# The values' part of the removals in one burst with the first corner product, its copies behind the corner copies

## The chip, the cores and the metric

One of the eight cores of a Trainium2 chip runs the whole program, and the metric is the device time of one execution in microseconds (us); lower is better. The core has a matrix engine (TensorE, PE in the profile, with its weight loads as PEld), VectorE (DVE), ScalarE (ACT) and GpSimd (POOL), each working through its own list of instructions in order, and SyncE (SP), whose list here is the DMA transfers that it issues. TensorE writes its results to banks of PSUM, from which the other engines read them.

## The reference

One step of a bidirectional hybrid layer on 128 context tokens and 256 latent tokens with 2048 channels. A normalised input is projected by `w_in`, 20,864 columns wide. One branch is an RWKV-7 time mixing in 32 heads of 64 channels, with a scan in each direction; the other a gated short convolution; both are projected, gated, merged and projected again. The scan, for each head and direction:

```python
def step(S, inp):
    r_t, w_t, k_t, v_t, a_t, b_t = inp
    sa = jnp.einsum('dbhij,dbhj->dbhi', S, a_t)
    S = S * w_t[..., None, :] + sa[..., :, None] * b_t[..., None, :] + v_t[..., :, None] * k_t[..., None, :]
    y = jnp.einsum('dbhij,dbhj->dbhi', S, r_t)
    return S, y
```

`sa` is the removal: what the state S gives for the key `a_t`, written back along `b_t` in the same step. The values `v_t` of earlier steps are in S too, and so they have a part in every later removal.

## The kernel before

**The stream.** `Stream` multiplies the input by the columns of `w_in`, 128 or 256 at a time. All matmuls are in a 32-bit format of reduced precision; to keep float32, each operand is split in a high and a low part, and a product is three matmuls (`mm3`, lines 81 to 83). A step of the stream is one `mm3` of 128 x 384. Weights come in loads of 1 MB on SyncE (`raw_*`, two buffers); from each, ScalarE casts two high parts (`whi_*`, line 88) and VectorE subtracts for two low parts (`wlo_*`, line 89), three buffers each. A load waits until the `wlo` of the load two before it is done. `ds_.go(n)` issues n steps.

**The blocks.** The scan runs in 16 blocks `b` of two heads. Each direction has six chunks of 64 tokens, so a block has 12 chunk products `f`, each for two heads `h`. A block is prepared and scanned while the stream goes on: every `yield n` in a preparing or scanning function is followed by n stream steps (`drive`). TensorE's order is thus written out by hand (`manual_schedule`). The other engines' lists are ordered by the scheduler, by estimated times and priorities: the scan has priority 300, all else 0.

**A block in order.** `prep_b` makes the score matrices on TensorE (`pA`), masks them into `A`, and sends the 32 x 32 diagonal blocks of the removals by DMA (`ui`) into `U`, where VectorE inverts them in 30 dependent pairs of steps (lines 721 and 723, about 29 us). ScalarE makes the transpose `UT` (line 727). `U` and `UT` go out to DRAM (`uo`, lines 728 and 729) and come back as blocks of `A` (line 734, four transfers) and as `x11` (line 735, two transfers, `x` in the profile). `prep_c` transposes values (`pv`) and keys (`pb`) and, at its end, computes `pav`: 24 products of 64 x 64, on TensorE as 48 passes, of the values in `sav[64:128]` with `A[64:128]`. ScalarE copies the two banks to `sav[0:64]` in four copies, and POOL clears `A[64:128, 0]` behind the products. Then `prep_a` of the next block loads two small weights (`lraw`, one buffer, line 621), splits them (`lwh` on ScalarE, `lwl` on VectorE, one buffer each), and multiplies by them (`pl`, four times) with stream steps between; `pn` is a product with two matmuls. At least 80 stream steps (`WINDOW`) after the start of `prep_c` the scan begins.

**The scan.** `corner("pH")` is 24 products of 32 x 32 (48 passes) of `A` and `x11`, copied back to `x11[32:64]` by ScalarE and VectorE in turn. `chain(1)` and `chain(0)` are the recurrences: `po` (state by scores), added onto `sav` on VectorE; `pq`, copied to `sav[0:64]` by ScalarE; `pu`, added to the state `st` by VectorE. `corner("pX")` is the second corner, copied to `A[0:32]`. `prep_k` of the next block is held back behind those copies by `issue_after`, which makes the scheduler put what is in its scope behind a given instruction. `py` is the output product.

**Banks.** `pl`, `pn`, `pav`, `pH`, `pX` and the recurrences share five PSUM banks in turn (`bank`). The stream has three of its own.

In the profile's names the numbers are left out: `wlo_bg` is a low weight part of the group `bg`, `d_bg` its result bank.

Of the kernel before, what the change touches and what calls it, by code (L numbers as in the profile page):

```python
# [15 lines left out]
P = 128  # L16
# [5 lines left out]
C = 64  # L22
NCH = 6
# [33 lines left out]
def hybrid_step(ctx, tc, cst, x_prompt, x_sample, state_f, state_b, c, c_ctx, ada_w, ada_b, norm_g,  # L57
# [3 lines left out]
    V, S, G, TE = nc.vector, nc.scalar, nc.gpsimd, nc.tensor  # L61
# [191 lines left out]
    def pcol(i, n=1):  # L253
        return par[:, i:i + n]
# [154 lines left out]
    def tmp(nm):  # L409
        return box["sp"].tile([P, T], F32, tag="t", name=nm, bufs=8)  # L410
# [177 lines left out]
    hss = [slice(0, C), slice(C, P)]  # L588

    def bank(nm):  # L590
        return ps1.tile([P, 4, P], F32, tag="A", name=nm, bufs=5)
# [4 lines left out]
    def flat(a):  # L596
        return a.rearrange("p n t -> p (n t)")
# [4 lines left out]
    def hl_parts(t, hi, nm):  # L602
        lo = sp.tile([P, T], F32R, tag="t", name=f"lo_{nm}", bufs=8)
        S.copy(hi[:], t[:])
        V.tensor_tensor(lo[:], t[:], hi[:].bitcast(F32), ALU.subtract)
        return hi, lo
# [130 lines left out]
    def prep_c(b, o):  # L737

        r, v, A = r_[b], v_[b], o["A"]

        s_in = sp.tile([P, 2, C], F32, tag="s_in", name=f"s_in_{b}")
        for d in range(2):
            for h in range(2):
                for jb in range(2):
                    p0 = C * h + 32 * jb
                    nc.sync.dma_start(s_in[p0:p0 + 32, d, :].rearrange("i (b j) -> i b j", j=32),
                                      ctx_st[d][0, 0, 2 * b + h].rearrange("(b i) j -> i b j", i=32)
                                      [:, :, 32 * jb:32 * jb + 32])

        sav = sp.tile([P, 2 * NCH, P], F32, tag="sav", name=f"sav_{b}")  # L750
        bt = sp.tile([P, 2 * NCH, P], F32, tag="bt", name=f"bt_{b}")
        o["sav"], o["bkt"] = sav, bt
        for d in range(2):
            if d == 0:
                src = v
            else:
                src = tmp(f"vr_{b}")
                S.copy(src[:], v[:, ::-1])
            pv = bank(f"pv_{b}_{d}")
            for q in range(3):  # L760
                TE.transpose(pv[:, q, :], src[:, q * P:(q + 1) * P], ident)
            for e in range(2):
                S.copy(sav[C:P, NCH * d + e:NCH * d + NCH:2, :], pv[C * e:C * e + C, 0:3, :])
            yield 1
        for d in range(2):

            for n0, n1 in (((0, 4), (4, 5)), ((0, 3), (4, 6)))[d]:
                pb = bank(f"pb_{b}_{d}_{n0}")
                for n in range(n0, n1):
                    TE.transpose(pb[:, n - n0, :], o["bk"][d][:, n, :], ident)  # L770
                S.copy(bt[:, NCH * d + n0:NCH * d + n1, :], pb[:, 0:n1 - n0, :])
                yield 1
        pvs = [bank(f"pav_{b}_{d}") for d in range(2)]
        for f in range(2 * NCH):
            for h in range(2):
                TE.matmul(flat(pvs[f // NCH][hss[h]])[:, C * (f % NCH):C * (f % NCH) + C], A[C:P, 0, f, hss[h]],
                          sav[C:P, f, hss[h]], start=True, stop=True)
        for d in range(2):
            for h in range(2):
                S.copy(sav[0:C, NCH * d:NCH * d + NCH, hss[h]],  # L780
                       flat(pvs[d][hss[h]])[:, 0:NCH * C].rearrange("p (n i) -> p n i", i=C))

        G.memset(A[C:P, 0, :, :], 0.0)
        yield 2
        ks = o["kd"]
        V.tensor_tensor(ks[0][:], ks[0][:], ks[1][:, ::-1], ALU.add)
        V.scalar_tensor_tensor(ks[0][:], ks[0][:], pcol(RK + b), r[:], ALU.mult, ALU.mult)
        o["bsum"] = hl_parts(ks[0], sp.tile([P, T], F32R, tag="t", name=f"bsh_{b}", bufs=8), f"bs_{b}")
        yield 1
        for h in range(2):  # L790
            for d in range(2):
                V.transpose(st[1][hss[h], d, hss[h]], s_in[hss[h], d, :])

    def scan(b, o):
        A, x11, sav, bt = o["A"], o["x11"], o["sav"], o["bkt"]
# [51 lines left out]
        def corner(nm, lhs, rhs):  # L847
            pz = bank(f"{nm}_{b}")
            for f in range(2 * NCH):
                for h in range(2):  # L850
                    g = 32 * (2 * (f % 2) + h)
                    TE.matmul(flat(pz[g:g + 32])[:, 32 * (f // 2):32 * (f // 2) + 32], lhs(f, h), rhs(f, h),
                              start=True, stop=True)
            return [flat(pz[32 * j:32 * j + 32])[:, 0:192].rearrange("p (n t) -> p n t", t=32) for j in range(4)]

        pz = corner("pH", lambda f, h: A[0:32, 0, f, C * h + 32:C * h + C], lambda f, h: x11[0:32, 2 * f + h, :])
        for j in range(4):
            (S.copy, V.tensor_copy)[j % 2](x11[32:64, j::4, :], pz[j])
        yield H0
        lat = chain(1)  # L860
        next(lat)
# [9 lines left out]
        pz = corner("pX", lambda f, h: x11[32:64, 2 * f + h, :], lambda f, h: A[32:64, 0, f, C * h + 32:C * h + C])  # L871
# [16 lines left out]
        for q in range(3):  # L888
            for h in range(2):
                for d in range(2):  # L890
                    for e in range(2):
                        f = 2 * q + e if d == 0 else NCH + 5 - 2 * q - e
                        TE.matmul(py[hss[e], q, hss[h]], A[:, 1, f, hss[h]], sav[:, f, hss[h]],
                                  start=d == 0, stop=d == 1)
# [43 lines left out]
    def drive(gen, prio=0, at=None, fn=None):  # L938
        n = i = 0
        while True:  # L940
            if i == at:
                fn()
            i += 1
            with tc.high_priority(offset=prio):
                u = next(gen, None)
            if u is None:
                return n
            ds_.go(u)
            n += u
# [6 lines left out]
    for b in range(NB):  # L956
        if b < NB - 1:
            if b > 0:
                ds_.urgent += [(add_rk, b + 1), (add_gv, b)]
        if b == NB - 2:  # L960
            ds_.fills += [(add_gv, NB - 1)] + [(add_ob, g) for g in range(8)]
        pb_gen = prep_b(b, cur)
        ds_.go(next(pb_gen))
        if prev is not None:
            finish(b - 1, prev)
        drive(pb_gen)
        n = drive(prep_c(b, cur))
        nxt = {}
        if b < NB - 1:
            while f"gv{b}" not in ds_.done:  # L970
                ds_.go(1)
                n += 1
            n += drive(prep_a(b + 1, nxt))
        w = WINDOW + (FIRST if b == 0 else LAST if b == NB - 1 else 0)
        if n < w:
            ds_.go(w - n)

        def keys():

            with tc.issue_after(cur["turn"][0]), tc.issue_after(cur["turn"][1]):  # L980
                prep_k(b + 1, nxt)

        drive(scan(b, cur), 300, 3 if b < NB - 1 else None, keys)
        norm(b, cur)
        prev, cur = cur, nxt
# [122 lines left out]
    for half in range(2):  # L1108
# [8 lines left out]
        for s in range(3):  # L1117
# [10 lines left out]
            if half == 1:  # L1128
                f = rsf[:, s, :]
# [37 lines left out]
```

## Time and profile before

| | |
|---|---|
| median of three runs | 2240.18 us (2237.89 to 2241.36) |
| the profiled execution | 2242.0 us |
| its span | 2240.2 us |
| TensorE clock granted in it | 0.996 |
| `pav` on TensorE, 16 blocks | 25.8 us busy |
| copies of `pav` on ScalarE, 64 | 30.4 us busy, 476 ns each |
| memset of `A` on POOL, 16 | 1374 to 1382 ns each |

The span is the time from the first to the last instruction of the profiled execution. A row of a timeline below has the start in us from the span's start, the length in us, the engine, the line, the operation, the tiles written and read, and the shape; `x4` means that four alike are put together, and the length is then from the first start to the last end. In brackets is how long the engine was idle before and what ended this. `SPq` is SyncE's list: the length there is that of issuing, not of the transfer. Matmuls overlap, so their spacing is read from start to start. The last number of a DMA row is the median time in us from issue to landing. Line numbers are those of the kernel before.

### The profile page before, as it was taken

The page shows a single profiled execution, that of the slowest core. Times are in us where ns is not written, and L with a number is a line of the kernel's source. Part 1 is how long each engine was busy: PE and PEld are TensorE (multiplying, and loading weights), DVE is VectorE, ACT ScalarE, POOL GpSimd, SP SyncE. Part 2 cuts the span into 40 slices and gives each one's busy share as a digit, 9 for nine tenths or more (in the row PEclk, how much of TensorE's full clock was granted, in tenths as well). Part 3 has the DMA queues.
Part 4 walks back from the last instruction along what each step waited for, and adds up shares of the span by engine and source line. Part 5 has one row for each costly group of instructions (what it writes and reads, how often), then busy time and mean ns, then how long its engine had stood idle before and what let it go on. Part 6 is the DMA issues. An engine that isn't in the chain of part 4 may idle for free.

```text
span 2240.2 us, 40545 instructions
## 1 busy us (share of the span) xinstructions
PE 2179.2 (97%) x16020; PEld 2064.9 (92%) x16020; DVE 1540.2 (69%) x3208; ACT 1044.3 (47%) x1800; POOL 116.5 (5%) x113
## 2 busy tenths in 40 slices
PE   5899999999999999999999999999999999999998
PEld 3588999999999999999999999999999999998988
DVE  3248567787777778777878787777777774444354
ACT  4245445454545454454545454546455543333333
POOL 2000010101010100000010101010100000000000
PEclk9999999999999999999999999999999999999999
DMA  9973544444444445443444434444445455886633
GB/s 335 346 211 116 147 129 133 111 120 125 112 125 120 113 117 132 115 132 103 124 109 133 111 110 134 112 118 140 120 121 143 146 179 162 292 281 230 221 132 113
DMA packets 440397, 339.97 MB, mean 152 GB/s; under 512 B 95552, under 2 KB 421776, under 8 KB 439312
## 3 DMA queue, kind: packets, MB, share of 16 engines
q1 hardware_dynamic: 438720, 335.63, 51.1%
q8 instruction: 126, 2.06, 0.4%
q10 hardware_dynamic: 432, 1.57, 0.2%
q14 instruction: 63, 0.52, 0.1%
q0 software_dynamic: 1056, 0.19, 0.1%
HBM read 307.37 MB, written 29.36 MB: 150 GB/s over the span
## 4 chain that ended last, share of the span: by engine, by line
PE 81%; DVE 8%; DMA 5%; ACT 3%; SPq 2%; issue 1%; POOL 0%; POOLq 0%; ACTq 0%; DVEq 0%
PE d_rk L81 4%; PE d_rk L83 4%; PE d_rk L82 4%; PE d_gv L81 3%; PE d_gv L82 3%; PE d_gv L83 3%; DMA raw_adah<-in_ada_w_dram 3%; PE pA L700 2%; PE d_oa L81 2%; PE d_oa L83 2%; PE d_oa L82 2%; PE d_bc L81 2%; PE d_mb L81 2%; PE d_bc L83 2%; PE d_bc L82 2%; PE d_bx L81 2%
## 5 line engine op out<-in xcount | busy, mean ns | idle before, releaser
L721 DVE TENSOR_TENSOR ut<-U 48x30 f32<-48x30 f32 (+14 forms) x480 | 154.6, 322 | 16.2 <-DMA U<-ui 4.1
L81 PE MATMUL d_rk<-h_hi,whi_rk 128*128 128x384 f32 x480 | 163.0, 340 | 0.6 <-ACT lst L554 0.6
L723 DVE TENSOR_TENSOR U<-U,ut 48x30 f32<-48x30 f32 (+14 forms) x480 | 154.5, 322 | 12.1
L81 PE MATMUL d_gv<-h_hi,whi_gv 128*128 128x384 f32 x480 | 161.0, 335 | 0.0
L83 PE MATMUL d_gv<-h_hi,wlo_gv 128*128 128x384 f32 x480 | 160.7, 335 | 0.0
L82 PE MATMUL d_gv<-h_lo,whi_gv 128*128 128x384 f32 x480 | 160.7, 335 | 0.0
L83 PE MATMUL d_rk<-h_hi,wlo_rk 128*128 128x384 f32 x480 | 160.4, 334 | 0.0
L82 PE MATMUL d_rk<-h_lo,whi_rk 128*128 128x384 f32 x480 | 160.4, 334 | 0.0
L88 ACT CAST whi_gv<-raw_gv 128x1024 fp32r<-128x1024 f32 (+1 forms) x64 | 64.0, 1000 | 139.6 <-PE d_rk L82 96.9
L88 ACT CAST whi_rk<-raw_rk 128x1024 fp32r<-128x1024 f32 x60 | 63.0, 1054 | 106.4 <-PE d_rk L82 31.7
L89 DVE TENSOR_TENSOR wlo_rk<-raw_rk,whi_rk 128x1024 fp32r<-128x1024 f32 x60 | 72.9, 1218 | 44.9 <-ACT whi_rk L88 39.7
L81 PE MATMUL d_gb<-h_hi,whi_gb 128*128 128x384 f32 x256 | 92.2, 360 | 0.0
L924 POOL TENSOR_TENSOR rs<-var,nhalf 128x6 f32<-128x6 f32 x16 | 21.2, 1325 | 1364.1 <-DVE var L922 1364.1
L81 PE MATMUL d_bc<-h_hi,whi_bc 128*128 128x384 f32 x256 | 92.2, 360 | 0.0
L81 PE MATMUL d_bg<-h_hi,whi_bg 128*128 128x384 f32 x256 | 92.1, 360 | 0.0
L81 PE MATMUL d_bx<-h_hi,whi_bx 128*128 128x384 f32 x256 | 92.1, 360 | 0.0
L81 PEld LDWEIGHTS d_rk<-h_hi,whi_rk 128*128 128x128 f32 x480 | 90.1, 188 | 1.8 <-ACT lst L554 0.9
L81 PE MATMUL d_ma<-h_hi,whi_ma 128*128 128x384 f32 x256 | 91.7, 358 | 0.0
L81 PE MATMUL d_ob<-ybh,whi_ob 128*128 128x384 f32 x256 | 88.9, 347 | 2.6 <-ACT whi_ob L88 2.1
L81 PEld LDWEIGHTS d_gv<-h_hi,whi_gv 128*128 128x128 f32 x480 | 90.5, 189 | 0.2
L82 PEld LDWEIGHTS d_gv<-h_lo,whi_gv 128*128 128x128 f32 x480 | 90.5, 188 | 0.0
L83 PEld LDWEIGHTS d_gv<-h_hi,wlo_gv 128*128 128x128 f32 x480 | 90.4, 188 | 0.0
(315 smaller groups left out, 6641.9 us busy)
## 6 DMA issues: line engine op xcount, KB each, us to landing
raw_adah<-in_ada_w_dram SPq DMA_DIRECT2D x64, 512.0 KB, 8.6
raw_rk<-in_w_in_dram SPq DMA_DIRECT2D x60, 512.0 KB, 5.3
raw_gv<-in_w_in_dram SPq DMA_DIRECT2D x60, 512.0 KB, 4.9
raw_ma<-in_w_in_dram SPq DMA_DIRECT2D x16, 1024.0 KB, 5.5
raw_mb<-in_w_in_dram SPq DMA_DIRECT2D x16, 1024.0 KB, 5.7
raw_bc<-in_w_in_dram SPq DMA_DIRECT2D x16, 1024.0 KB, 5.5
raw_bx<-in_w_in_dram SPq DMA_DIRECT2D x16, 1024.0 KB, 5.4
raw_bg<-in_w_in_dram SPq DMA_DIRECT2D x16, 1024.0 KB, 5.5
```

What stands on the lines that cost most here:

```text
L81: TE.matmul(out, wh, xh, start=start, stop=False)
L82: TE.matmul(out, wh, xl, start=False, stop=False)
L83: TE.matmul(out, wl, xh, start=False, stop=stop)
L88: S.copy(hi[0:rows], src)
L89: V.tensor_tensor(lo[0:rows], src, hi[0:rows].bitcast(F32), ALU.subtract)
L700: TE.matmul(pas[h, n // 4 * 4][:, n % 4, :], bk[hss[h], n, :], pr[hss[h], n, :], start=True, stop=True)
L721: V.tensor_tensor(tv, U[:, 0:s, s:s + 1].broadcast_to([48, s, w]), U[:, s:s + 1, s + 1:].broadcast_to([48, s, w]), ALU.mult)
L723: V.tensor_tensor(U[:, 0:s, s + 1:], U[:, 0:s, s + 1:], tv, ALU.add)
L924: G.tensor_tensor(rs[:], var[:], nhalf[:], ALU.pow)
```

## The change

The 24 products of `pav`, the four copies, the memset and a `yield 2` leave `prep_c`. The products now stand at the start of `scan`, directly ahead of `corner("pH")` without a stream step between; the copies are issued behind the last ScalarE copy of `pH` (`issue_after(xs.ins)`); the memset follows. What the two stream steps of the removed `yield 2` did, the loop ahead of `prep_a` or the padding up to `WINDOW` does.

```diff
@@ prep_c
                 S.copy(bt[:, NCH * d + n0:NCH * d + n1, :], pb[:, 0:n1 - n0, :])
                 yield 1
-        pvs = [bank(f"pav_{b}_{d}") for d in range(2)]
-        for f in range(2 * NCH):
-            for h in range(2):
-                TE.matmul(flat(pvs[f // NCH][hss[h]])[:, C * (f % NCH):C * (f % NCH) + C], A[C:P, 0, f, hss[h]],
-                          sav[C:P, f, hss[h]], start=True, stop=True)
-        for d in range(2):
-            for h in range(2):
-                S.copy(sav[0:C, NCH * d:NCH * d + NCH, hss[h]],
-                       flat(pvs[d][hss[h]])[:, 0:NCH * C].rearrange("p (n i) -> p n i", i=C))
-
-        G.memset(A[C:P, 0, :, :], 0.0)
-        yield 2
         ks = o["kd"]
@@ scan
+        pvs = [bank(f"pav_{b}_{d}") for d in range(2)]
+        for f in range(2 * NCH):
+            for h in range(2):
+                TE.matmul(flat(pvs[f // NCH][hss[h]])[:, C * (f % NCH):C * (f % NCH) + C], A[C:P, 0, f, hss[h]],
+                          sav[C:P, f, hss[h]], start=True, stop=True)
+        xs = None
         pz = corner("pH", lambda f, h: A[0:32, 0, f, C * h + 32:C * h + C], lambda f, h: x11[0:32, 2 * f + h, :])
         for j in range(4):
-            (S.copy, V.tensor_copy)[j % 2](x11[32:64, j::4, :], pz[j])
+            x = (S.copy, V.tensor_copy)[j % 2](x11[32:64, j::4, :], pz[j])
+            xs = x if j % 2 == 0 else xs
+        with tc.issue_after(xs.ins):
+            for d in range(2):
+                for h in range(2):
+                    S.copy(sav[0:C, NCH * d:NCH * d + NCH, hss[h]],
+                           flat(pvs[d][hss[h]])[:, 0:NCH * C].rearrange("p (n i) -> p n i", i=C))
+
+        G.memset(A[C:P, 0, :, :], 0.0)
         yield H0
```

The scheduler orders the other engines anew. SyncE's list in block 6, from the way out of the inverse on (`x_6` is `x11` of block 6, `raw_gb` a weight load of the stream, `lraw_0` the first small weight of the preparation in block 7), before:

```order
L728 DMA uo_8519<-U_8614 48x1024
L729 DMA uo_8519<-UT_8678 48x1024
L734 DMA A_8520<-uo_8519 32x12x32 x2
L735 DMA x_6_8682<-uo_8519 32x12x32
L734 DMA A_8520<-uo_8519 32x12x32 x2
L735 DMA x_6_8682<-uo_8519 32x12x32
L101 DMA raw_gb_0_9216<-in_w_in_dram 128x8x256
L101 DMA raw_gb_1_9370<-in_w_in_dram 128x8x256
L621 DMA lraw_0_10223<-in_w_dram 96x2x128
```

and now:

```order
L101 DMA raw_gb_0_9216<-in_w_in_dram 128x8x256
L728 DMA uo_8519<-U_8614 48x1024
L729 DMA uo_8519<-UT_8678 48x1024
L621 DMA lraw_0_10192<-in_w_dram 96x2x128
L734 DMA A_8520<-uo_8519 32x12x32 x2
L735 DMA x_6_8682<-uo_8519 32x12x32
L734 DMA A_8520<-uo_8519 32x12x32 x2
L735 DMA x_6_8682<-uo_8519 32x12x32
L101 DMA raw_gb_1_9370<-in_w_in_dram 128x8x256
```

The first `raw_gb` has moved ahead of `uo`, and `lraw_0` ahead of the four `A` and two `x` transfers. The even blocks 2 to 12 have this order; the odd blocks keep theirs; in block 15 a weight load stands between `uo` and `A` that was behind `x`.

VectorE's list at the end of the inverse of block 6 (`ut` and `U` are its steps, `ga` a gate, `wlo_bg` low weight parts), before:

```order
L721 TENSOR_TENSOR ut_8616<-U_8614 48x58
L723 TENSOR_TENSOR U_8614<-U_8614,ut_8616 48x29x2
L721 TENSOR_TENSOR ut_8616<-U_8614 48x30
L723 TENSOR_TENSOR U_8614<-U_8614,ut_8616 48x30
L89 TENSOR_TENSOR wlo_bg_0_1_9006<-raw_bg_0_8999,whi_bg_0_1_9005 128x1024
L440 TENSOR_TENSOR ga_9045<-ga_9045,d_gv_0_8938 128x384
```

and now:

```order
L721 TENSOR_TENSOR ut_8616<-U_8614 48x58
L89 TENSOR_TENSOR wlo_bg_0_1_8975<-raw_bg_0_8968,whi_bg_0_1_8974 128x1024
L723 TENSOR_TENSOR U_8614<-U_8614,ut_8616 48x29x2
L721 TENSOR_TENSOR ut_8616<-U_8614 48x30
L723 TENSOR_TENSOR U_8614<-U_8614,ut_8616 48x30
L440 TENSOR_TENSOR ga_9014<-ga_9014,d_gv_0_8907 128x384
```

A `wlo_bg` that stood behind the last step of `U` now stands inside the chain. On ScalarE, `ga` goes from behind `UT` to ahead of it in the even blocks, and one `whi` cast does so in the odd ones.

TensorE's list where the scan of block 6 begins (`pn` is the end of the next block's preparation), now:

```order
L633 MATMUL pn_9129<-sqh_9041,bones_r 128x384
L634 MATMUL pn_9129<-lo_sq_9042,bones_r 128x384
L848 MATMUL pav_0_9135<-sav_8698,A_8520 64x64 x12
L848 MATMUL pav_1_9136<-sav_8698,A_8520 64x64 x12
L840 MATMUL pH_9161<-x_6_8682,A_8520 32x32 x24
L81 MATMUL d_bg_1_9052<-h_hi_77,whi_bg_0_1_8974 128x384
```

The two `pav` rows stood between stream steps at the end of `prep_c` before, and `pH` followed `pn` directly. (The list counts a product of two passes once, so 24 rows here are 48 matmuls in the profile.)

## The prediction

> **What bounds the kernel now.** I read the busy table first, then the chain that ended last, then TensorE's waits.
>
> ```profile
> PE 2179.2 (97%) x16020; PEld 2064.9 (92%) x16020; DVE 1540.2 (69%) x3208; ACT 1044.3 (47%) x1800; POOL 116.5 (5%) x113
> ...
> PE 81%; DVE 8%; DMA 5%; ACT 3%; SPq 2%; issue 1%; POOL 0%; POOLq 0%; ACTq 0%; DVEq 0%
> ```
>
> TensorE is busy for 97% of the span and has 81% of the chain. Its order is written by hand and holds the same matmuls after the change, so the time changes in two ways only: what it costs to go from one kind of matmul to another, and how long TensorE stands still. Its waits in the blocks are small today (columns: waited in total, times, longest):
>
> ```profile
> PE po L814 <- DVE st L843: 5.3, 7, 1.2
> PE pu L838 <- ACT sav L833: 4.4, 11, 0.5
> ...
> PE pl L83 <- DVE lwl L89: 1.7, 1, 1.7
> ...
> PE pH L852 <- DMA x<-uo: 0.2, 1, 0.2
> ```
>
> The last two rows matter most: `pl` and `pH` almost never wait today. The question is whether they still do not when TensorE reaches them sooner and the engines that feed them are reordered. I work block 6 through and carry it to the others.
>
> **The burst itself.** TensorE around the old place of `pav`, then around `pH`:
>
> ```profile
> 852.55 0.34 PE L83 MATMUL d_rk<-h_hi,wlo_rk 128*128 128x384 f32 x1
> 852.82 1.61 PE L776 MATMUL pav<-sav,A 64*64 64x64 f32 x48
> 854.36 0.45 PE L81 MATMUL d_rk<-h_hi,whi_rk 128*128 128x384 f32 x1
> 854.65 0.34 PE L82 MATMUL d_rk<-h_lo,whi_rk 128*128 128x384 f32 x1
> ...
> 892.86 0.34 PE L83 MATMUL pl<-l_hi,lwl 96*128 96x384 f32 x1
> ...
> 895.86 0.34 PE L634 MATMUL pn<-lo_sq,bones_r 128*128 128x384 f32 x1
> 896.13 0.62 PE L852 MATMUL pH<-x,A 32*32 32x32 f32 x48
> 896.68 0.44 PE L81 MATMUL d_bg<-h_hi,whi_bg 128*128 128x384 f32 x1
> 896.96 0.33 PE L82 MATMUL d_bg<-h_lo,whi_bg 128*128 128x384 f32 x1
> ```
>
> Stream matmuls follow each other at 0.17 us (854.65 to 854.82 in step). `pav` takes 0.27 to enter, 1.54 to its successor's start, and that successor needs 0.29: 2.10. Without it two steps of 0.17 remain, 0.35. So from the old place to `pH` TensorE runs **1.75 us earlier**. At the new place one entry of 0.27 serves both products. The 47 intervals of `pav` are 0.030 each, from (1.61 − 0.22)/47 with one matmul at 0.22, so 1.40, plus one step from `pav` to `pH`, which no row shows. Bounds: 0.03, as inside a burst, and 0.27, as on entry. The nearest row is the way out of `pav`, 1.54 − 1.40 = 0.14, and I take it: the new place costs **1.54 us**. Balance −0.21 us a block, −3.4 us in 16 (−5.1 to −1.3 by the bounds).
>
> The Trainium skill ("TensorEngine Tiling (Array Packing)", Key Properties) says that a change of tiling mode drains TensorE, and `pav` runs in 64*64 tiles, `pH` in 32*32, so this burst still holds a change. The trace agrees where it can: an entry takes 0.27, not 0.17. By that rule the step stands near 0.27, and the sum would come out 2.1 us higher.
>
> **What the 1.75 us meet.** `pl` needs `lwl` from VectorE, `pH` needs `x` from DMAs. In block 6 these hang on the inverse `U`, whose steps fill VectorE without a gap until it ends:
>
> ```profile
> 884.41 0.21 DVE L723 TENSOR_TENSOR U<-U,ut 48x30 f32<-48x30 f32 x1
> 884.54 1.21 DVE L89 TENSOR_TENSOR wlo_bg<-raw_bg,whi_bg 128x1024 fp32r<-128x1024 f32 x1
> ...
> 888.39 1.23 DVE L89 TENSOR_TENSOR wlo_bg<-raw_bg,whi_bg 128x1024 fp32r<-128x1024 f32 x1 [0.62 <-ACT whi_bg L88]
> ...
> 891.31 0.42 DVE L89 TENSOR_TENSOR lwl<-lraw,lwh 96x256 fp32r<-96x256 f32 x1
> ```
>
> ```profile
> 884.66 2.14 ACT L727 COPY UT<-U 48x1024 f32<-48x1024 f32 x1 [0.51 <-DVE U L723]
> 886.69 0.49 ACT L439 ACTIVATE ga<-d_gv 128x384 f32<-128x384 f32 x1
> 887.30 1.05 ACT L88 CAST whi_bg<-raw_bg 128x1024 fp32r<-128x1024 f32 x1
> ```
>
> In the new order the first `wlo_bg` stands inside the `U` chain (second excerpt of the change), so `U` ends 1.14 us later (its 1.21 less the overlap of neighbours), at 885.76, and `UT` runs to 887.9. `ga` goes ahead of `UT` on ScalarE, which gives back 887.30 − 886.69 = 0.61. The second `whi_bg`, and the second `wlo_bg` that waits for it, come 1.14 − 0.61 = 0.5 to 0.6 later; the ops between it and `lwl` follow without a gap, so `lwl` ends not at 891.73 but near **892.3**. TensorE wants it at 892.86 − 1.75 = 891.11: a stall of about 1.2 us where 1.13 was spare. The removed ScalarE copies give nothing back here, as they ended 29 us before `UT` (853.78 + 1.93):
>
> ```profile
> 853.78 1.93 ACT L780 COPY sav<-pav 64x384 f32<-64x384 f32 x4
> ```
>
> The second wait is on SyncE, whose rows are today:
>
> ```profile
> 849.23 0.44 SPq L716 DMA_DIRECT2D U<-ui  x1
> ...
> 884.65 0.34 SPq L728 DMA_DIRECT2D uo<-U  x1
> 886.82 0.33 SPq L729 DMA_DIRECT2D uo<-UT  x1
> ...
> 890.00 0.98 SPq L734 DMA_DIRECT2D A<-uo  x2
> 891.03 0.47 SPq L735 DMA_DIRECT2D x<-uo  x1
> 891.54 3.71 SPq L101 DMA_DIRECT2D raw_gb<-in_w_in_dram  x2
> 895.30 0.58 SPq L621 DMA_DIRECT2D lraw<-in_w_dram  x1
> ```
>
> ```profile
> x<-uo SPq DMA_DIRECT2D x2, 48.0 KB, 2.0
> ```
>
> In the new order `lraw` of the next block stands ahead of the `A` and `x` transfers (first excerpt). Its single buffer is read by `lwl`, so it waits for 892.3, takes 0.58, and behind it stand four `A` and two `x`: twice 0.98 and twice some 0.4 with gaps, so the last `x` is issued near 895.4 instead of 891.03 and lands 2.0 later, at **897.4**. Undisturbed, `pH` would start at 896.13 − 1.75 + 1.54 = 895.92, and its second half, which needs that `x`, 0.2 later. With the stall at `pl` alone that half stands at 897.3, with the `x` alone at 897.4: the two waits lie beside each other and are not added. Against 896.33 today it is **+1.1 us**. The order is alike in blocks 2, 4, 8, 10 and 12, some with less spare in the transfers; I take 1.3 for each of the six: +7.8. The wait for `lwl` also holds whatever is behind `lraw` on SyncE, which is just these six transfers and the next weight load.
>
> What bounds this: if `lwl` came the full 1.75 earlier with TensorE, neither wait would form, −0.2 a block; if every delay added (1.2 + 1.1), +2.3 a block.
>
> **Odd blocks.** There the `U` chain is as before. In blocks 5 and 9 `lwl` has no spare today:
>
> ```profile
> 787.48 0.42 DVE L89 TENSOR_TENSOR lwl<-lraw,lwh 96x256 fp32r<-96x256 f32 x1
> ```
>
> ```profile
> 787.96 0.44 PE L83 MATMUL pl<-l_hi,lwl 96*128 96x384 f32 x1
> ```
>
> `lwl` ends at 787.90 and `pl` starts at once. One ScalarE cast of about 1.0 us moves from behind `UT` to ahead of it, so `lwl` can come some 0.95 earlier, not 1.75: `pl` at 787.0, then 1.54 for the burst, `pH` +0.55. Two blocks: +1.1. Block 13 is alike but loses a late `x` of today: 0. Blocks 0, 1, 3, 7, 11 and 14 keep spare and gain 0.21 each: −1.3.
>
> **Block 15.** A 1 MB weight load moves to between `uo` and `A`, as block 7 has it now:
>
> ```profile
> 992.52 0.39 SPq L101 DMA_DIRECT2D raw_bg<-in_w_in_dram  x1
> ...
> 996.34 1.28 SPq L735 DMA_DIRECT2D x<-uo  x1
> ```
>
> ```profile
> x<-uo SPq DMA_DIRECT2D x2, 48.0 KB, 4.5
> ```
>
> ```profile
> 1844.08 1.23 DVE L89 TENSOR_TENSOR wlo_ob<-raw_ob,whi_ob 128x1024 fp32r<-128x1024 f32 x1 [3.10 <-ACT whi_ob L88]
> ```
>
> ```profile
> 1851.58 0.62 PE L852 MATMUL pH<-x,A 32*32 32x32 f32 x48
> ```
>
> In block 7 the last `x` lands 7.5 to 8.3 us after that load is issued (3.8 to its issue, then 3.7 to 4.5, the median of two). In block 15 the load waits for the `wlo_ob` that ends at 1845.31, so `x` lands near 1852.9; `pH`'s second half stands at 1851.8 today: +1.2.
>
> **The moved copies.** Four ScalarE copies of 0.48 us (1.93 us in each block) now follow the two ScalarE `x` copies. The second of these and VectorE's first add onto `sav`, which now also waits for the moved copies, are today:
>
> ```profile
> 897.52 0.31 ACT L858 COPY x<-pH 32x192 f32<-32x192 f32 x1 [0.42 <-DVE x L858]
> ```
>
> ```profile
> 899.02 0.42 DVE L815 TENSOR_TENSOR sav<-po,sav 64x256 f32<-64x256 f32 x1 [0.80 <-PE po L814]
> ```
>
> The add stands 2.9 us after `pH`'s start. The `x` copy ends 1.7 after it, and with 1.93 more the moved copies end 3.6 after it. So the add comes 0.8 later; TensorE then runs stream steps, and the products that read this part of `sav` come after the second corner product, so I cost it at nothing; without that cover it is up to 0.6 us a block. Behind the copies on ScalarE are a weight cast and the second corner's copies, which wait for later products. POOL's 1.38 us memset runs beside this; POOL is 5% busy.
>
> **Sum.** +7.8 + 1.1 + 0 + 1.2 − 1.3 = **+8.8 us** on the profiled execution (2242.0 us around a span of 2240.2). That execution lies 1.8 above the median, 2240.18, on which I set the sum: **2249.0 us**.
>
> **Rivals.**
> 1. *The waits do not form.* The order on ScalarE and VectorE is fixed, but if each chain keeps its 1.1 us lead because its inputs also come 1.75 earlier, only the burst's saving is left: 2240.2 − 3.4 = 2236.8, and 2235.1 with a step of 0.03. For it: weight casts are released by TensorE. Against it: the transfer that `U` starts from leaves at 849.23, ahead of the old place of `pav` at 852.82, and the chain has no gap to give up. The deciding point is `lwl` at 891.1 in block 6: earlier, and this one holds. It is faster, or too little to be measured.
> 2. *Half of it.* `lraw` or the `U` chain costs only 0.5 to 0.6 us a block (`lwl` at 891.8): 6 × 0.5 + 0.5 + 1.2 − 1.5 = +3.2: 2243.4.
> 3. *The scan pays too.* `pu` waits already, 0.5 at the longest (row above). If the late add pushes the recurrences, 0.3 to 0.6 us a block, so 5 to 9 us more, 2254 to 2258.
> 4. *Nothing changes.* The step from `pav` to `pH` is 0.27 and the odd blocks only balance the even: about 2240; counted with the second.
>
> **How the numbers follow.** Forecast 0.54 (own range 2245 to 2253), first rival 0.14, second with the fourth 0.20, third 0.12. Differences within 0.2%, 4.5 us, are about what a measurement of this kernel can tell from no change: the bounds are 2235.7 and 2244.7. Faster: 0.08, the better half of the first rival. Same: 0.06 of the first and 0.14 of the second, 0.20. Slower: 0.72. The range goes from 2237.5, which leaves out the first rival but for its edge, to 2256, in the middle of the third: some 0.18 outside.
>
> **What would show it.** In the new profile `pav` and `pH` stand in one burst, 1.5 us between their starts; the `pl` row waits for `lwl` by about 1.2 us in even blocks; `lraw` is issued ahead of `A`; `pH` waits on `x<-uo` there. `U` ends 1.1 us later in even blocks and as before in odd ones. I am wrong if `pl` and `pH` show no waits, or if the difference lies in `po`, `pu` or `pq`.

## The result and the profile after

The change made the kernel slower: 2252.78 us median of six runs (2250.02 to 2260.21) against 2239.87 (2237.89 to 2241.88), a ratio of 1.0062 with a 95% interval of 1.0046 to 1.0079. The forecast was 2249.0 with a range of 2237.5 to 2256. The profiled execution took 2256.05 us around a span of 2254.2.

The page of the kernel after, busy times and the chain that ended last:

```profile
PE 2184.5 (97%) x16020; PEld 2069.4 (92%) x16020; DVE 1538.6 (68%) x3208; ACT 1042.9 (46%) x1800; POOL 115.4 (5%) x113
...
PE 70%; DVE 15%; DMA 5%; ACT 4%; issue 3%; SPq 2%; POOL 0%; POOLq 0%; DVEq 0%; ACTq 0%
```

The counts are the same; in the chain TensorE's share fell from 81 to 70%, and VectorE's rose from 8 to 15%. TensorE's waits after (total, times, longest):

```profile
PE po L802 <- DVE st L831: 7.2, 9, 1.6
PE pl L83 <- DVE lwl L89: 6.7, 9, 1.7
PE pH L840 <- DMA x<-uo: 3.1, 5, 1.2
PE pl L81 <- ACT lwh L88: 1.7, 4, 0.7
PE pu L826 <- ACT sav L821: 1.4, 6, 0.2
```

`pl` and `pH`, which waited 1.7 and 0.2 us before, now wait 8.4 and 3.1 (1.7 of `pl`, before and after, is one wait ahead of the blocks); `po` rose by 1.9 and `pu` fell by 3.0. Block 6 again, which begins 5.29 us later than before (first `pA` at 843.44 for 838.15). VectorE, then TensorE:

```profile
889.14 1.21 DVE L89 TENSOR_TENSOR wlo_bg<-raw_bg,whi_bg 128x1024 fp32r<-128x1024 f32 x1
...
890.74 0.21 DVE L723 TENSOR_TENSOR U<-U,ut 48x30 f32<-48x30 f32 x1
...
896.99 0.41 DVE L89 TENSOR_TENSOR lwl<-lraw,lwh 96x256 fp32r<-96x256 f32 x1
```

```profile
897.46 0.44 PE L83 MATMUL pl<-l_hi,lwl 96*128 96x384 f32 x1 [0.64 <-DVE lwl L89]
...
900.82 1.61 PE L848 MATMUL pav<-sav,A 64*64 64x64 f32 x48
902.67 0.91 PE L840 MATMUL pH<-x,A 32*32 32x32 f32 x48 [0.23 <-DMA x<-uo]
```

The `wlo` runs inside the `U` chain, `lwl` ends at 897.40 and `pl` starts at 897.46; the burst then waits for `x` between and within its products. SyncE's rows and the transfer of `x` (KB, median us to landing, in the stretch 896 to 906):

```profile
890.37 0.37 SPq L101 DMA_DIRECT2D raw_gb<-in_w_in_dram  x1
890.98 0.39 SPq L728 DMA_DIRECT2D uo<-U  x1
893.11 0.33 SPq L729 DMA_DIRECT2D uo<-UT  x1
897.44 0.33 SPq L621 DMA_DIRECT2D lraw<-in_w_dram  x1
897.88 0.90 SPq L734 DMA_DIRECT2D A<-uo  x2
898.82 0.47 SPq L735 DMA_DIRECT2D x<-uo  x1
899.33 0.98 SPq L734 DMA_DIRECT2D A<-uo  x2
900.35 1.20 SPq L735 DMA_DIRECT2D x<-uo  x1
```

```profile
x<-uo SPq DMA_DIRECT2D x2, 48.0 KB, 3.3
```

SyncE stands from 893.44 to 897.44 before `lraw`, until `lwl` is done, with six transfers behind it.

Where the time went is read best from two distances on TensorE, block by block: from the first `pA` to the first `pH`, and from there to the next `pA`. The stretch from `pA` of block 0 to `pH` of block 15 was 1665.27 us and is 1679.30, +14.0:

| part | change, us |
|---|---|
| `pA` to `pH`, blocks 2, 4, 6, 8, 10, 12 | +1.24, +1.11, +1.25, +1.47, +1.24, +3.26 |
| `pA` to `pH`, blocks 1, 3, 7, 11, 14 | −0.18 each |
| `pA` to `pH`, blocks 0, 5, 9, 13, 15 | −0.25, +0.32, +1.01, −0.34, +0.72 |
| `pH` to next `pA`, blocks 0 to 14 | +3.91 |

Of the last row 2.5 are waits inside `pH` in blocks 2, 4 and 6, and 1.2 a stretch of block 2 at half clock (last section); what is left, +0.2, is the recurrences, which lose in some blocks what they gain in others.

### The profile page after: what moved, and what is told of

It reads as the page before. It is cut to its first block, busy times and chain, and to the rows that moved or that the text cites. A ratio compares the mean times of both kernels' runs of the same rounds, so it can differ in the third digit from the quotient of the medians.

```text
span 2254.2 us, 40569 instructions
## 1 busy us (share of the span) xinstructions
PE 2184.5 (97%) x16020; PEld 2069.4 (92%) x16020; DVE 1538.6 (68%) x3208; ACT 1042.9 (46%) x1800; POOL 115.4 (5%) x113
## 3 DMA queue, kind: packets, MB, share of 16 engines
q10 hardware_dynamic: 432, 1.57, 0.2%
## 4 chain that ended last, share of the span: by engine, by line
PE 70%; DVE 15%; DMA 5%; ACT 4%; issue 3%; SPq 2%; POOL 0%; POOLq 0%; DVEq 0%; ACTq 0%
DMA raw_adah<-in_ada_w_dram 3%; PE d_rk L81 3%; PE d_rk L82 3%; PE d_rk L83 3%; PE d_gv L81 3%; PE d_gv L82 3%; PE d_gv L83 3%; PE pA L700 2%; PE d_oa L81 2%; PE d_oa L83 2%; PE d_oa L82 2%; PE d_mb L81 2%; PE d_mb L83 2%; PE d_mb L82 2%; PE d_bc L81 2%
## 5 line engine op out<-in xcount | busy, mean ns | idle before, releaser
L81 PE MATMUL d_mb<-h_hi,whi_mb 128*128 128x384 f32 x256 | 90.4, 353 | 0.0
```

The costliest lines, as they stand in the source:

```text
L81: TE.matmul(out, wh, xh, start=start, stop=False)
```

## The experiments

Three theories stood against each other: (1) TensorE comes earlier while the engines that feed it were reordered, so `pl` and `pH` wait; (2) the copies behind the corner copies delay the scan; (3) the burst itself costs, since the tile size changes in it. All runs in one table. The ratio is taken over all executions of a run and of the kernel before beside it, so it need not be the quotient of the two medians (most apart in e9, 1.0101). The stretch is that from `pA` of block 0 to `pH` of block 15 in the profiled execution, against the kernel before:

| run | median, us | before beside it | ratio, 95% interval | stretch, us |
|---|---|---|---|---|
| the change | 2252.78 | 2239.87 | 1.0062, 1.0046 to 1.0079 | +14.0 |
| e1_lraw_behind_x | 2251.54 | 2241.28 | 1.0050, 1.0036 to 1.0064 | +7.4 |
| e2_u_whole | 2246.43 | 2241.28 | 1.0025, 1.0016 to 1.0034 | +3.1 |
| e5_before_lraw_first | 2250.70 | 2241.28 | 1.0044, 1.0029 to 1.0059 | +8.8 |
| e7_copies_free | 2255.97 | 2241.28 | 1.0073, 1.0059 to 1.0086 | +16.0 |
| e9_small_two | 2262.15 | 2239.51 | 1.0089, 1.0074 to 1.0104 | +21.7 |
| e10_u_whole_small_two | 2240.12 | 2239.51 | 1.0003, 0.9994 to 1.0012 | −2.0 |
| e11_best | 2239.14 | 2239.51 | 1.0000, 0.9991 to 1.0009 | +2.3 |
| e12_before_small_two | 2240.53 | 2239.51 | 1.0000, 0.9991 to 1.0009 | +0.5 |
| e13_loads_behind_x | 2239.41 | 2240.09 | 0.9992, 0.9984 to 1.0001 | −0.0 |
| e14_same_copies_free | 2237.57 | 2240.09 | 0.9984, 0.9975 to 0.9992 | −1.8 |
| e15_one_step_between | 2248.02 | 2240.09 | 1.0032, 1.0020 to 1.0043 | +8.9 |

Stretch and median need not agree: the stages ahead of and behind the blocks differ by some 3 us between profiled executions (the first `pH` of block 0 lies up to 3.5 us earlier than before), and the median is over other executions too.

### One order forced on SyncE: lraw behind x

```diff
+with (tc.issue_after(xd[b - 2].ins) if m == 0 and b > 2 else ExitStack()):
     nc.sync.dma_start(lraw[:], ...)
```

Here `b` is the block being prepared, whose load is issued two blocks ahead, and `xd[b - 2]` is the last transfer into `x11` of the block that then runs.

> The changed kernel, with one order forced: the next block's small weight load (lraw) is issued behind the A and x transfers of the block instead of ahead of them. The U chain keeps the wlo inside it. Theory 1 (the two waits come from the new order on SyncE and VectorE): the waits of pH on x, 3.1 us in the profile after, go, and with them the stretch at half clock behind the longest of them, some 1.3 us; the waits of pl on lwl stay. 2252.8 - 4.4 = about 2248.5. Theory 2 (the copies moved behind the corner copies delay the scan): no change, 2252 to 2253. Theory 3 (the burst itself costs, by the change of tile size in it): no change, 2252 to 2253.

TensorE's waits in it:

```profile
PE pl L83 <- DVE lwl L89: 6.8, 10, 1.7
...
PE pH L842 <- DMA x<-uo: 1.0, 2, 0.8
```

The wait of `pH` fell from 3.1 to 1.0 (all of that in block 15), that of `pl` for `lwl` stayed, as theory 1 said. The median fell by only 1.2 us where 4.4 were expected (2.6 when each is set against the kernel before beside it), and its interval overlaps that of the change, so the times alone do not show a gain. The profiled stretch is 6.6 less, but the profiled execution of the change lay 3.3 above its median. So by the waits the order of `lraw` is part of the cost, but `pl` alone still holds most of it.

### One order forced on VectorE: the U chain whole

```diff
+ul = V.tensor_tensor(U[:, 0:s, s + 1:], U[:, 0:s, s + 1:], tv, ALU.add)
+if 1 < b < 15:
+    ud[b] = ul.ins
...
+with (tc.issue_after(behind) if behind is not None else ExitStack()):
     V.tensor_tensor(lo[0:rows], src, hi[0:rows].bitcast(F32), ALU.subtract)
```

`behind` is `ud[b]` for the second low part of the first load after the group `gv`, and none else.

> The changed kernel, with one order forced in blocks 2 to 14: the low weight part that the new order put inside the U chain is issued behind the chain's last step. SyncE's list, ordered anew, then has lraw behind the A and x transfers too. Theory 1: the waits of pl and of pH in the six even blocks go, 6 x 1.2 us by the distances from pA to pH, 2 us more in block 12 and about 3 in block 2, where the clock fell to half; what is left is the burst's saving, some 0.2 us a block, against the waits in blocks 5, 9 and 15: 2239 to 2241. Theory 2: the copies still stand behind the corner copies, so 2251 to 2253. Theory 3: 2251 to 2253.

```profile
PE pl L83 <- DVE lwl L90: 4.8, 8, 1.7
...
PE pH L846 <- DMA x<-uo: 1.1, 2, 0.9
```

Theory 1 has the direction: 6.4 us less than the change (7.8 against the kernel before beside each), while the burst and the copies stayed. As expected, SyncE's list has `lraw` behind `x` in this run, so both new orders are gone and not VectorE's alone; one weight load of the stream still stands between `uo` and `A` in the even blocks. The median is 5 above the forecast, and the rows say where: `pl` still waits 4.8 us, 3.1 of it in the blocks. With the chain whole `lwl` ends 0.3 us earlier in block 6 than in the kernel before, counted from its `pA`, but TensorE comes 1.75 us sooner, and the spare was 1.13. The even blocks are still 0.2 to 0.8 longer from `pA` to `pH`. So the earlier arrival itself is a third source of the cost, beside the two orders.

### The old kernel with the new order of lraw

```diff
+for i_ in ad[b - 2]:
+    tc.add_manual_dep(i_, lrd.ins.name, mybir.DependencyInfo(...NoSync, ...), reason="order")
```

`ad[b]` holds the `A` and `x` transfers of block b, and `lrd` is the issue of `lraw`. It applies to blocks 2 to 12, the even ones; the second of the weight loads behind them is put behind `x` too.

> The kernel before, pav in its old place, with one order forced in the even blocks 2 to 12: lraw of the next block is issued ahead of the A and x transfers. U chain and copies as before. Theory 1: lraw waits for lwl (ends at 891.73 in block 6), takes 0.6, the last x is issued some 2.9 later and lands 2.0 to 2.6 after that, at 897.2 to 897.8, where pH's second half wants it at 896.3: 0.9 to 1.5 us a block, 5 to 9 in six, so 2245 to 2249, and pH's rows wait for x. Theories 2 and 3: no change, 2240.

TensorE's wait, then block 6 on SyncE and TensorE:

```profile
PE pH L862 <- DMA x<-uo: 5.8, 7, 1.9
```

```profile
890.90 0.33 SPq L627 DMA_DIRECT2D lraw<-in_w_dram  x1
...
893.82 0.47 SPq L744 DMA_DIRECT2D x<-uo  x1
```

```profile
897.61 0.39 PE L862 MATMUL pH<-x,A 32*32 32x32 f32 x24 [1.95 <-DMA x<-uo]
```

This is the strongest evidence: with `pav` and the copies in their old places, the new order on SyncE costs 9.4 us (2245 to 2249 were expected, 2250.7 measured). The order is not quite that of `lraw` alone: the scheduler also put the first 1 MB weight load of the even blocks between `uo` and `lraw`. That load alone does not make the wait: the run with the `U` chain whole and two buffers, below, has it there too, with `lraw` behind `x`, and `pH` waits in none of these blocks. The single waits, 0.5 to 2.1 us, are larger than reckoned in blocks 6 and 10: in 6 the last `x` lands 3.7 us after its issue (2.1 to 2.5 in the other even blocks), and in 10 an issue of `A` ahead of it takes 1.57 us instead of 0.46. In block 6 half the clock follows (0.50 from 898.28 on), which is part of the 9.4.

### The copies ahead of the corner copies

```diff
+        for d in range(2):
+            for h in range(2):
+                S.copy(sav[0:C, NCH * d:NCH * d + NCH, hss[h]], ...)
         xs = None
...
-        with tc.issue_after(xs.ins):
-            for d in range(2):
-                for h in range(2):
-                    S.copy(sav[0:C, NCH * d:NCH * d + NCH, hss[h]], ...)
```

> The changed kernel, with the four copies of pav issued directly behind the products, ahead of the corner copies on ScalarE; pav stays in one burst with pH, and SyncE's list keeps lraw ahead of A and x in the even blocks. Theory 1: within 1.5 us of the changed kernel, 2251.3 to 2254.3. Theory 2: the adds onto sav come 0.8 us sooner and the scan is freed of 0.3 to 0.6 us a block, 2243 to 2248. Theory 3: no change, 2252 to 2253.

2255.97, 3 us above the change in the medians, 1.8 against the kernel before beside each, with intervals that overlap: theory 2, which expected 2243 to 2248, falls. In its undisturbed blocks (1, 7, 11, 14) the distance from `pH` to the next `pA` is that of the kernel before to 0.02 us, while behind the corner copies it was 0.24 shorter in blocks 1, 12 and 14, 0.8 shorter in 7 and 11 and 0.6 to 1.0 longer in 0, 5, 9 and 10. The sum is about nothing. If it is slower than the change at all, the waits of `pH` on `x` can account for it, 4.9 us for 3.1; SyncE's order in the even blocks is the same in both.

### Two buffers for the split small weights

```diff
-lwh, lwl = split(lraw[:], [96, 2, P], "lwh", "lwl", sp, f"{b}_{m}", rows=96)
+lwh, lwl = split(lraw[:], [96, 2, P], "lwh", "lwl", sp, f"{b}_{m}", rows=96, bufs=2)
```

Four kernels have it: the change alone (e9), with the `U` chain whole (e10), with a weight load of block 15 behind `x` besides (e11), and the kernel before (e12).

> The changed kernel with two buffers instead of one for the split small weights (lwh, lwl). Each lwl is then made a half block ahead of its pl, so that pl no longer waits at the end of the U chain; in VectorE's and SyncE's lists the lwl and the load at the old places are those of the next use, so in the even blocks a small load that waits for lwl still stands ahead of the A and x transfers, and a wlo still stands in the U chain. Theory 1 (two waits that lie beside each other): the waits of pl go, also in blocks 5 and 9 (1.3 us together), but pH waits for x longer in their place in all six even blocks, 1.5 to 2 us each; 2249 to 2252. Rival (the wait of pl alone is the cost, x follows from it): 2239 to 2241.

```profile
PE pH L841 <- DMA x<-uo: 13.3, 11, 2.3
```

No row of `pl` is left, and `pH` waits 13.3 us in its place. The rival expected 2239 to 2241; 2262.15 is also 10 above theory 1's forecast, as `pH` waits 0.9 to 3.0 us in each of the six even blocks and a stretch at half clock follows in five of them, twice as long as usual in three. The two waits do lie beside each other: without the first, the second shows in full.

> The changed kernel with both: the wlo behind the U chain in blocks 2 to 14, and two buffers for lwh and lwl. The moved products and copies stay as in the change. Theory 1: pl and pH wait nowhere but in block 15 (1.3 us); every block from pA to pH is 0.18 us shorter than in the kernel before, 2.7 us in 15; against 2241.3 that is 2239 to 2241. Rival (the products and copies cost in the scan themselves, as what was left in the run with the U chain whole, 2246.4, may say): 2245 to 2247.

Block 6 in it:

```profile
890.55 1.61 PE L855 MATMUL pav<-sav,A 64*64 64x64 f32 x48
892.10 0.62 PE L847 MATMUL pH<-x,A 32*32 32x32 f32 x48
```

2240.12, as expected. `pl` waits nowhere, `pH` only in block 15; `pA` to `pH` is 0.18 us shorter than before in every block from 1 to 14, and 0.2 to 0.55 in the three (5, 9, 13) where `pl` was late or had least to spare. Burst and copies are those of the change, so theory 3 falls too, and the 12.7 us between this run and the change were all in the order and the lead of the feeding engines.

> As the run before, and in block 15 the weight load that the new order put between uo and A is issued behind x. Theory 1: the wait of pH in block 15, 1.3 us, goes: 2238 to 2239.5, some 2 us under the kernel before, about what can just be told. Rival: if something else is late there, no difference to the run before.

2239.14, but not for the reason expected: the wait in block 15 is gone, and instead `x` was 1.3 and 1.4 us late in blocks 4 and 8 of the profiled execution. In the even blocks of this run and of the one before, a weight load stands between `uo` and `A` and leaves `x` little spare: the last one landed 0.4 us ahead of its use in block 6 of the run before, and here 3.3 and 3.8 us after its issue was done in blocks 4 and 8, for 1.5 to 2.6 in the even blocks of the run before. The median cannot be told from the kernel before.

> Control: the kernel before with two buffers for lwh and lwl. Theory 1: its waits of pl are 0.3 us in block 5 and 0.2 in block 13, so 0.5 us less at most, 2240.5 to 2241.5. Rival (the buffers help by themselves): under 2239.

2240.53 with a ratio of 1.0000: the buffers alone give nothing that can be measured.

### The loads behind x again, the place of the copies, and a step between

Three kernels, all with the `U` chain whole, the two buffers, and the scan's weight loads issued behind `x` in the even blocks and block 15. The first keeps the copies behind the corner copies; the second has them ahead; the third has one stream step between `pav` and `pH`:

```diff
+        yield 1
         pz = corner("pH", ...)
...
-        yield H0
+        yield H0 - 1
...
-        drive(scan(b, cur), 300, 3 if b < NB - 1 else None, keys)
+        drive(scan(b, cur), 300, 4 if b < NB - 1 else None, keys)
```

The last pair keeps the next block's `prep_k` at its place in the scan, which has one `yield` more.

> The changed kernel with the wlo behind the U chain, two buffers for lwh and lwl, and in the even blocks and block 15 the weight loads of the scan issued behind x, as SyncE's list had them before the change. The burst and the copies stay as in the change. Theory 1 (all the loss came from the order of the feeding engines and from the lead that TensorE takes on them): no wait at pl or pH in any block; from pA of block 0 to pH of block 15 it is 2.5 to 4 us shorter than in the kernel before (16 x 0.2, and 0.5 for the waits of pl that it had); 2236.5 to 2239, 1 to 3 us under the kernel before. Rival (the scan pays for the copies): that stretch no shorter than before, 2240 or more.

2239.41, not told from the kernel before (its interval reaches 1.0001), and 0.4 above the range expected. `pl` and `pH` wait nowhere; blocks 0 to 14 are 3.15 us shorter from `pA` to `pH`. The gain is given back in block 15, 2.3 us longer in this execution (waits at `pv` and `pb`, 2.5 us for 1.4 before, and half the clock from 1795.04 on), and in the scan, 0.8.

> As the run before, but with the copies of pav directly behind the products, ahead of the corner copies. Theory 1: within 1 us of the run before, as what the scan gains in one block it loses in another. Rival (the place of the copies behind the corner copies costs): 2 us or more faster than the run before; the opposite (their place behind is worth something): 1.5 us or more slower.

```profile
PE po L814 <- DVE st L843: 5.4, 6, 1.2
PE pu L838 <- ACT sav L833: 3.6, 9, 0.5
```

2237.57, a ratio of 0.9984 with an interval that excludes 1: this version is the only one of those here that is faster than the kernel before, by 0.16%, which is less than the 0.2% that the prediction counted as no change. It is 1.8 us under the run before it, between the two expectations, and the intervals overlap. In the profiles the difference lies in block 15 and not in the scans (+1.35 here, +0.81 there): `pv` waits alike, 1.72 us here and 1.75 there, but only there did half the clock follow. Whether the place of the copies is worth anything stays open.

> As the first run of these three, but with one stream step between pav and pH, so that they are no longer one burst; all else in place. The saving of the burst by itself: leaving pav and entering pH anew costs 0.15 + 0.29 + 0.17 + 0.27 = 0.88 where three steps and 0.15 are 0.67: 0.21 us a block, 3.3 in 16. Theory 1: 3 to 4 us slower than the first run, 2240 to 2242, like the kernel before. Rival (the change of tile size eats the saving): no difference to the first run.

`pA` to `pH` became 0.73 us longer than in the first of the three, in nearly every block: one step of 0.52 and **0.21** for leaving and entering anew, as reckoned. But 2248.02 is far above the 2240 to 2242 expected. The rest of the 8.6 us lies behind `pH`: the step moved ahead is missing there, and the way to the next `pA` should be 0.52 shorter a block, but in the sum it is as long as in the first run:

```profile
PE po L814 <- DVE st L843: 6.8, 15, 1.1
...
PE pq L831 <- DVE sav L815: 1.6, 3, 0.5
...
PE d_bg L81 <- DVE bc L473: 1.2, 3, 0.4
```

`po` waits 15 times instead of 6 in the other two, and stream steps wait for results of VectorE. So this run confirms the size of the burst's saving by the distances, not by its total.

## Why the prediction was right

Term by term, in the profiled execution:

- **The burst.** Forecast −0.21 us a block, measured −0.18 in the undisturbed blocks. The unknown step from `pav` to `pH` was taken at 0.14, and is 0.15 (890.55 to 892.10 above, less 1.40 for the 47 intervals). The Trainium skill's sentence on a change of tiling mode ("TensorEngine Tiling (Array Packing)", Key Properties) gives no size; the prediction read it as a step near the entry's 0.27, and the measurement decides against that size.
- **`U`, `UT`, `lwl` in block 6.** Less the 5.29 us of shift, `U` ends at 885.66 (forecast 885.76), `lwl` at 892.11 (892.3), `pl` starts at 892.17. The stall is 1.06 where 1.2 was forecast.
- **SyncE in block 6.** The last `x` is issued at 895.06 (895.4). It landed not 2.0 but about 2.8 us later (`pH`, 0.91 long for 0.62 and begun 0.3 late, waited for both `x`), so that the burst waited again.
- **The six even blocks.** Forecast +7.8. Measured +9.6 to `pH`, 2.5 more inside `pH`, and 1.2 at half clock behind it in block 2; of the 9.6, block 12 has 2 more than the others, 1.5 of them at half clock behind a longer wait of `pl`. "The two waits lie beside each other and are not added" was the step that failed in part: it held in blocks 8, 10 and 12, and in 2, 4 and 6 the wait for `x` came on top, by 0.6 to 1.4 us, because the last `x` landed later than summed. The term that was mis-sized is not one and the same: in block 6 it is the transfer (2.8 us for 2.0), in blocks 2 and 4 (2.35 and 2.18) mostly an issue of `A` on SyncE, which took 1.78 and 1.23 us instead of 0.47.
- **Odd blocks and block 15.** Blocks 5 and 9: +1.33 for +1.1 (by its own terms −0.95 + 1.54 = 0.59 each, so 1.2). Block 13: −0.34 for 0. Block 15: +0.72 to `pH` and 0.45 inside it, for +1.2 (its 1852.9 less 1851.8 is 1.1). The other six: −1.15 for −1.3.
- **The copies.** Forecast nothing, and about nothing in the sum, though not in each block (−1.3 to +1.0 where nothing else is late). The first add onto `sav` comes 0.83 us later, counted from `pH`, as forecast (0.8).

The sum was +8.8 against 12.9 in the medians. The reasons were right; what was missing is the later `x` (2.5) and the half clock (2.7), together about 5 us of the profiled 14. The half clock behind a wait has no term in the prediction at all.

Rival 1 asked for `lwl` at 891.1 and got 892.1; rival 3's late recurrences did not appear. One point of the argument was too mild: the run with the chain whole, where `lwl` was not late and `pl` still waited, says that `pl` would have waited without any reordering, for its spare of 1.13 us is less than the 1.75 by which TensorE came sooner.

## What to carry to other kernels

Taking work off an engine that is busy nearly all the time moves everything behind it forward, and each feeder's spare there has to exceed that shift; read those spares, in both distances and queues, before counting the saving. A change in one engine's hand-written order also reorders the engines that a scheduler orders, and one transfer that waits for a late result holds everything issued behind it on the same queue. The saving of three microseconds, 0.18 a block for 0.21 reckoned, was there in the distances, but only after the order of two queues and one pair of buffers had been put right, and even then the total told it from the kernel before in one of four runs.

## What the runs showed of the hardware

A wait of TensorE in the burst was followed by half its clock. Block 2 of the kernel after, TensorE, and then by windows (us, busy time and count of each engine, granted clock, DMA share, GB/s):

```profile
477.21 0.55 PE L840 MATMUL pH<-x,A 32*32 32x32 f32 x24 [1.24 <-DMA x<-uo]
477.69 0.69 PE L81 MATMUL d_bg<-h_hi,whi_bg 128*128 128x384 f32 x1
478.18 0.52 PE L82 MATMUL d_bg<-h_lo,whi_bg 128*128 128x384 f32 x1
478.50 0.52 PE L83 MATMUL d_bg<-h_hi,wlo_bg 128*128 128x384 f32 x1
```

```profile
475.58:477.21 1.63, 0.39 (x26) 0.28 (x24) 0.00 (x0) 0.00 (x0) 1.37 (x1) 1.00 0.78 82
477.21:480.71 3.50, 3.50 (x33) 3.44 (x34) 0.71 (x2) 2.41 (x6) 0.00 (x0) 0.51 0.96 314
480.71:483.00 2.29, 2.29 (x16) 2.21 (x15) 0.62 (x2) 1.38 (x4) 0.00 (x0) 1.00 0.05 12
```

After a wait of 1.24 us the clock is 0.51 over the next 3.5 us, and stream matmuls follow at 0.32 us instead of 0.17. In the kernel before a wait of the same length at `po` does no such thing:

```profile
605.45 0.68 PE L814 MATMUL po<-st,pr 128*128 128x128 f32 x4 [1.16 <-DVE st L843]
```

```profile
604.10:605.45 1.35, 0.19 (x3) 0.04 (x1) 1.29 (x4) 0.06 (x1) 0.00 (x0) 1.00 0.14 18
605.45:609.00 3.55, 3.55 (x23) 3.55 (x24) 3.46 (x7) 1.54 (x3) 0.00 (x0) 1.00 0.32 70
```

Where the wait lies in time counts too. In each trace the half-clock stretches begin whole multiples of 3.413 us apart (in the kernel after at 173.47, 477.26, 1535.39 and 1866.48, which are 89, 310 and 97 such steps), so TensorE's idle time can be counted in pieces of that length. The pieces that hold the two waits above:

```profile
473.85:477.26 3.41, 2.17 (x78) 1.83 (x79) 0.89 (x2) 0.88 (x2) 1.37 (x1) 1.00 0.67 85
```

```profile
602.83:606.24 3.41, 2.25 (x15) 1.96 (x14) 3.29 (x8) 0.69 (x2) 0.00 (x0) 1.00 0.11 14
```

TensorE is idle for 1.24 and 1.16 us in them, and half clock follows only the first. Over the blocks of all thirteen traces, a piece at full clock that held `pav` or `pH` was followed by half clock in all 17 cases with 1.02 us or more of idle time, and in none with 1.01 or less. Of the pieces without such small tiles none was in 22 cases with 1.02 to 1.36 us, and four were in nine cases with 1.39 to 2.08. A wait that lies across two pieces counts in parts: `pH` in block 10 of the old kernel with the new order waited 1.70 us, 0.69 in one piece and 1.01 in the next, without half clock. So the small tiles ahead of a wait seem to count toward it; that is a reading of these cases and was not tried by itself. The Trainium skill ("TensorE: Matmul & The Clock Gate", Part 1) names an idle window of about 3.4 us as what halves the clock, and the same length of work as what restores it: the 3.5 us of recovery agree, the 1.24 us of wait do not. The half clock also goes with the spread of the runs of the change, 10 us where those of before spread over 4: the granted clock was 0.997 in the execution of 2250.02 us, 0.995 in that of 2256.05 and 0.993 in that of 2260.21.
